# Norms of q and k and the softmax's inverse sums by way of DRAM, in a two-layer hybrid diffusion block

## The chip, the cores and the metric

The kernel runs on one core of a Trainium2 chip. A core has a matrix engine (TensorE, PE in the profile), three engines that work element by element (VectorE or DVE, ScalarE or ACT, GpSimd or POOL), and SyncE (SP), which here does nothing but issue DMA transfers. Each engine has its own list of instructions and works through it in order; semaphores hold an instruction back until what it needs is done. The metric is the device time of one execution, in microseconds (us).

## What is computed

Two layers work on 256 context tokens followed by 256 latent tokens, 1024 features wide. Each layer norms its input, projects it to the inputs of three branches (a state-space branch, SSD; neighbourhood attention; a gated MLP), sums the gated branches, projects, and ends with a SwiGLU block. The last layer returns the latent tokens only. The parts that matter here are the norm of q and k per head and the softmax:

```
def qkv_heads(t, q_norm, k_norm):
    q, k, v = [u.reshape(Bt, L, NA_HEADS, NA_HEAD_DIM) for u in split_cols(t, (NA_WIDTH,) * 3)]
    return rmsnorm(q, q_norm), rmsnorm(k, k_norm), v          # 8 heads of 64
...
    p = jax.nn.softmax(jnp.concatenate([s_lat, s_ctx], axis=3).astype(jnp.float32), axis=3)
    out = einsum(p_lat, v_win) + einsum(p_ctx, vc)            # latent queries
    ...
    p = jax.nn.softmax(s.astype(jnp.float32), axis=-1)        # context queries, layer 0 only
```

## The kernel before

Activations lie with features on the 128 partitions and the 512 tokens along the free dimension (context in columns 0 to 255, latent in 256 to 511). Layer 1 needs the context only for k, v and the SSD states, so most of its products are 256 columns wide.

Weights are streamed once, in the order of use, in 316 loads of 512 KB (tile `wr`, five buffers shared with another stream, `wm`). For each, ACT makes a high part (`hi`, L222) and DVE the remainder (`lo`, L232), and every product is three matmuls: high by high, high by low, low by high. A load is issued by SP once DVE has made the low part that frees its buffer.

All work is written in one fixed order by hand. The products of the weights are the main line; each of them calls `tick`, and at each tick three queues of side work (`ssd`, `att`, `mod`) move one or more steps forward (one `yield` of a generator is a step). `later(dt, fn)` puts a piece of work off by dt ticks. So the order of every engine, SP's too, is fixed when the program is built, and a wait of an instruction holds everything behind it on its engine.

`qk_norm` runs in the `att` queue, four times: k and q in each layer. The squares of four tiles (two heads in each) are summed by heads with a small matmul into 32 rows for each of the four tiles; ACT takes the root, DVE inverts it (`rq`, two halves), a high and a low part are put into `RQ`, and for each tile a matmul with a constant selector (`selp`) spreads two heads' rows over 64 partitions each, into PSUM. DVE multiplies q or k by it (L1094). Between these stand fixed numbers of steps: Q_0, Q_1 and Q_2.

`attention` follows in the same queue. For each head, `scores_lat` or `scores_ctx` makes the scores, their maximum, and on ACT the exponentials with their sums (`bt` for latent queries, two tiles of 128x512; `pc` for context queries, two halves of 128x256). Half a tick later DVE inverts the sums and scales the exponentials (L1148 to L1150, L1169 to L1172). Two steps after its scores a head's probabilities are transposed on PE (`transp`, L1186), and four steps after them `pv_out` multiplies two heads by v, and ACT and DVE split the result into `yna` (tiles `ynh`, `ynl`; `ynp` in layer 1; L1202, L1203). There are 16 such heads in layer 0 (8 of the context, 8 of the latent tokens) and 8 in layer 1.

The SSD branch already sends small rows through DRAM: `Fd` and `Cd` are stored from `R`, and `fetch` loads two rows of `Fd`, repeated on all partitions, into `rb`, from which DVE makes a mask `M` one step later (L896).

Of the kernel before, what the change touches and what calls it, by code (L numbers as in the profile page):

```python
# [33 lines left out]
C_ROW = 1280  # L34
# [61 lines left out]
def kernel(ctx: ExitStack, tc: tile.TileContext, a, out):  # L96
# [19 lines left out]
    def T(s="t", dt=F32):  # L116
        return tpool.tile([128, TOK], dt, tag="t", name=nm(s))

    def S(s="s"):
        return pspool.tile([128, 512], F32, tag="p", name=nm(s))  # L120
# [25 lines left out]
    selp = cpool.tile([128, 8, 128], F32R, name="selp")  # L146
    lom = cpool.tile([128, 1], F32, name="lom")
# [227 lines left out]
    def table(func):  # L375

        ACT.activation(dummy, epsb, func)
# [227 lines left out]
    for l in range(NL):  # L605
# [39 lines left out]
        if not last:  # L645
            SP.dma_start(out=cst[:, 0:C_ONE], in_=a["cst"][:, 0:C_ONE])
            SP.dma_start(out=cst[:, C_COS:C_ROW], in_=a["cst"][:, C_COS:C_ROW])
            SP.dma_start(out=cst[:, C_BS:C_MF], in_=a["cst"][:, C_BS:C_MF])
            SP.dma_start(out=mk, in_=a["cst"][:, C_MF:NC_])
            DVE.tensor_copy(selp.rearrange("p a (b c) -> p a b c", c=64),  # L650
                            cst[:, C_SP:C_SP + 16].rearrange("p (a b) -> p a b", b=2).unsqueeze(3).to_broadcast(
                                [128, 8, 2, 64]))

            DVE.tensor_reduce(out=lom, in_=cst[:, C_ROW + 4:C_ROW + 8], op=ADD, axis=AX.X)
            DVE.tensor_scalar(lom, lom, -1.0, None, MUL)
# [119 lines left out]

        def pair_rows(j, pr):

            return selp[:, 2 * j + pr]
# [287 lines left out]
        def qk_norm(kind):  # L1066
# [7 lines left out]
            rq, RQ = T("rq"), T("RQ", F32R)  # L1074
            if kind == "q":
                ACT.activation(rq[:, b:], ps[:, b:], AF.Sqrt, bias=eps64)
            else:
                ACT.activation(rq[:, b:], ps[:, b:], AF.Sqrt, scale=1.0 / 64, bias=epsb)
            table(AF.Exp)
            for c in range(b, 512, 256):  # L1080
                DVE.reciprocal(rq[:, c:c + 256], rq[:, c:c + 256])
                yield
            for _ in range(Q_1[l]):
                yield

            ACT.copy(RQ[:, b:], rq[:, b:])
            DVE.scalar_tensor_tensor(RQ[:, b:], RQ[:, b:].bitcast(F32), lom, rq[:, b:], MUL, ADD)
            for _ in range(Q_2[l]):
                yield
            for j in range(4):  # L1090
                ps = S()
                mm(ps[:, b:], pair_rows(j, 0), RQ[:, b:])
                t = qk[kind, j]
                DVE.scalar_tensor_tensor(t[:, b:], t[:, b:], pcol(P_KN if kind == "k" else P_QN),  # L1094
                                         ps[:, b:], MUL, MUL)
                yield

        def attention():
# [34 lines left out]

            def scores_lat(hd):
# [12 lines left out]
                def rest():  # L1147
                    DVE.reciprocal(st_[:, 6:8], st_[:, 4:6])  # L1148
                    for qt in (0, 1):
                        DVE.tensor_scalar(pr[qt], pr[qt], st_[:, 6 + qt:7 + qt], None, MUL)  # L1150

                later(A_N[l], rest)
                return pr

            def scores_ctx(hd):
# [12 lines left out]
                def rest():  # L1168
                    DVE.reciprocal(st_[:, 6:8], st_[:, 4:6])  # L1169
                    for qt in (0, 1):  # L1170
                        sl = slice(qt * 256, qt * 256 + 256)
                        DVE.tensor_scalar(p[:, sl], p[:, sl], st_[:, 6 + qt:7 + qt], None, MUL)  # L1172

                later(A_N[l], rest)
# [17 lines left out]
            def pv_out(s_, j, pts):  # L1192
# [9 lines left out]
                ACT.copy(hi[:, sl], ps[:, 0:256])  # L1202
                DVE.tensor_tensor(lo[:, sl], ps[:, 0:256], hi[:, sl], SUB)  # L1203
# [484 lines left out]
```

## Time and profile before

| | |
|---|---|
| median of 3 runs | 1604.22 us (1604.22 to 1604.6) |
| the profiled execution, its own time | 1605.74 us |
| its span, from the first instruction to the last | 1603.7 us |
| TensorE busy | 1581.2 us |
| DVE busy | 1162.3 us |
| ACT busy | 830.3 us |
| granted TensorE clock, mean | 0.997 of full speed |

Busy times are those of the engines' instructions; ends of matmuls are modelled, so that TensorE's figure also covers some time in which it is not at its peak. SP's work is the issue of transfers and is not counted.

### The profile page before, as it was taken

To read this page: it belongs to the slowest core of one execution; us is meant where nothing else is said; L and a number is where in the kernel's file an instruction comes from. 1 tells how busy PE (TensorE), PEld (TensorE's weight loads), DVE (VectorE), ACT (ScalarE), POOL (GpSimd) and SP (SyncE) were. 2 spreads that over 40 slices of the span, in tenths; PEclk is the share of its full clock that TensorE was granted. 3 is DMA by queue.
4 is the path that set the end of the run, shared out by engine and by line. 5 is a ranking of instruction groups with operands and counts; after the bars stand their busy time and mean duration, and the time that the engine had idled before them with its cause. 6 is when DMAs were issued, how large, how long until landed. Compare 5 with 4: busy or idle time off the path is not lost.

```text
span 1603.7 us, 23594 instructions
## 1 busy us (share of the span) xinstructions
PE 1581.2 (99%) x8908; PEld 1324.2 (83%) x8909; DVE 1162.3 (72%) x2005; ACT 830.3 (52%) x1551; POOL 6.9 (0%) x21
## 2 busy tenths in 40 slices
PE   9999999999999999999999999999999999999999
PEld 5878787767788888988888888978888989998888
DVE  5477889878968656666666654778988987687664
ACT  4456876646743234433222212658676775566652
POOL 0000000000000000000000000000000000000000
PEclk9999999999999999999999999999999999999999
DMA  9523333443344445455456765425434455656654
GB/s 347 190 61 122 115 107 107 154 153 99 113 130 127 157 144 178 133 171 166 162 184 206 261 231 177 171 93 161 132 118 138 140 158 178 204 163 196 187 173 135
DMA packets 87345, 254.37 MB, mean 159 GB/s; under 512 B 10560, under 2 KB 19008, under 8 KB 87104
## 3 DMA queue, kind: packets, MB, share of 16 engines
q1 hardware_dynamic: 87232, 252.87, 49.3%
q8 instruction: 70, 1.15, 0.3%
q14 instruction: 43, 0.35, 0.1%
HBM read 248.44 MB, written 4.39 MB: 158 GB/s over the span
## 4 chain that ended last, share of the span: by engine, by line
PE 78%; DVE 11%; ACT 5%; DMA 4%; issue 2%; SPq 0%; ACTq 0%; DVEq 0%
PE g L126 70%; PE s L126 6%; DVE lo L232 3%; DVE xbc L718 2%; DMA wm<-in_wmod 1%; ACT hi L222 1%; DMA rb<-Fd 1%; PE s L1186 1%; ACT M L987 1%; DVE scr L192 1%; DMA wr<-in_ws 1%; DVE bt L1141 0%; DVE M L896 0%; ACT rb L987 0%; ACT sw L740 0%
## 5 line engine op out<-in xcount | busy, mean ns | idle before, releaser
L126 PE MATMUL g<-hh,hi 128*128 128x512 f32 (+1 forms) x1280 | 471.0, 368 | 0.0
L126 PE MATMUL g<-hh,lo 128*128 128x512 f32 (+1 forms) x1280 | 462.0, 361 | 1.4 <-DVE lo L232 1.4
L126 PE MATMUL g<-hl,hi 128*128 128x512 f32 (+1 forms) x1280 | 461.8, 361 | 0.5 <-DVE hl L551 0.4
L232 DVE TENSOR_TENSOR lo<-wr,hi 128x1024 fp32r<-128x1024 f32 x316 | 382.5, 1219 | 92.9 <-ACT hi L222 92.7
L222 ACT CAST hi<-wr 128x1024 fp32r<-128x1024 f32 x316 | 323.7, 1046 | 38.8 <-DMA wr<-in_ws 36.0
L126 PEld LDWEIGHTS g<-hh,hi 128*128 128x128 f32 x1280 | 241.5, 189 | 48.7 <-issue 11.9
L126 PEld LDWEIGHTS g<-hh,lo 128*128 128x128 f32 x1280 | 241.5, 189 | 41.1 <-DVE lo L232 3.8
L126 PEld LDWEIGHTS g<-hl,hi 128*128 128x128 f32 x1280 | 241.7, 189 | 37.2 <-DVE hl L551 1.1
L192 DVE SCALAR_TENSOR_TENSOR scr<-wm,csil 128x1024 bf16<-128x1024 f32 x128 | 156.1, 1220 | 55.4 <-DMA wm<-in_wmod 55.4
L126 PE MATMUL g<-hp,hi 128*128 128x512 f32 x304 | 107.6, 399 | 0.0
L718 DVE SCALAR_TENSOR_TENSOR xbc<-g,pv,xbc 128x508 f32<-128x508 f32 (+3 forms) x128 | 91.3, 713 | 9.5 <-ACT xbc L712 6.4
L126 PE MATMUL g<-hp,lo 128*128 128x256 f32 x304 | 85.6, 282 | 0.9 <-DVE lo L232 0.8
L1295 ACT ACTIVATE th<-g,pv 128x512 f32<-128x512 f32 (+1 forms) x48 | 27.9, 581 | 95.3 <-PE g L126 89.6
L367 ACT CAST fh<-f 128x512 fp32r<-128x512 f32 x22 | 13.6, 620 | 112.3 <-DVE f L1446 112.3
L126 PE MATMUL g<-fh,lo 128*128 128x512 f32 x176 | 68.6, 390 | 0.5 <-DVE lo L232 0.5
L126 PEld LDWEIGHTS g<-hp,hi 128*128 128x128 f32 x304 | 57.1, 188 | 14.1
L126 PE MATMUL g<-fh,hi 128*128 128x512 f32 x176 | 68.5, 389 | 0.0
L126 PE MATMUL g<-fl,hi 128*128 128x512 f32 x176 | 68.5, 389 | 0.0
L126 PE MATMUL g<-lo,hh 128*128 128x256 f32 x224 | 63.6, 284 | 3.2 <-DVE lo L232 3.1
L126 PE MATMUL g<-hi,hh 128*128 128x256 f32 x224 | 64.6, 288 | 0.0
L126 PE MATMUL g<-hi,hl 128*128 128x256 f32 x224 | 63.3, 283 | 0.0
L126 PE MATMUL g<-fp,hi 128*128 128x512 f32 (+1 forms) x198 | 62.4, 373 | 0.0
(310 smaller groups left out, 2658.2 us busy)
## 6 DMA issues: line engine op xcount, KB each, us to landing
wr<-in_ws SPq DMA_DIRECT2D x316, 512.0 KB, 4.2
wm<-in_wmod SPq DMA_DIRECT2D x80, 512.0 KB, 4.5
rb<-Fd SPq DMA_DIRECT2D x48, 256.0 KB, 4.0
wm<-in_wm SPq DMA_DIRECT2D x32, 256.0 KB, 6.0
ex<-Cd SPq DMA_DIRECT2D x32, 128.0 KB, 3.8
bias<-in_rpb SPq DMA_DIRECT2D x32, 128.0 KB, 2.1
x<-in_xT SPq DMA_DIRECT2D x8, 256.0 KB, 5.1
xm<-in_xT SPq DMA_DIRECT2D x8, 256.0 KB, 5.5
```

Of the source, the lines that this page charges most:

```text
L126: PE.matmul(o, l, r, start=start, stop=stop)
L192: DVE.scalar_tensor_tensor(scr, raws[n], 1.0, csil[:, v, :], MUL, MUL, accum_out=modr[l][:, ft, v:v + 1])
L222: ACT.copy(hi, self.raw[i])
L232: DVE.tensor_tensor(lo, self.raw.pop(i), hi, SUB)
L367: ACT.copy(hi, src[:, c0:])
L718: DVE.scalar_tensor_tensor(av3[:, :, o0:o1], pv3[:, :, o0 + d:o1 + d], w(j), av3[:, :, o0:o1], MUL, ADD)
L987: ACT.activation(z, z, AF.Exp, bias=bias(st, d))
L1186: PE.transpose(ps[:, kt * 256 + qt * 128:kt * 256 + qt * 128 + 128], src, ident)
L1295: ACT.activation(th[:, c0:], ps[:, c0:], AF.Tanh, scale=0.5, bias=pcol(P_BG + br * 8 + m))
```

## The change

In the norms, the summed squares are copied out of PSUM as they are, and the two useful rows of each tile are stored to DRAM (`Nd`, four stores). They come back laid out over all 128 partitions, 32 numbers in each (`rqs`; 16 for q in layer 1), are rooted and inverted there, go to DRAM again, and are loaded for each tile, every row repeated on 64 partitions (`RQ`, two loads by `spread`). DVE multiplies by that tile in SBUF. The selector matmuls, the constant `selp` and the splitting are gone; the two steps between the halves of the reciprocal are gone too.

In attention, the inverse sums of a head (two numbers on each of 128 partitions) are stored to DRAM by `inverse` (tile `Pd`, one row of 256 numbers), and loaded back as a row repeated on 64 partitions (`inv`). The probabilities stay as they are; `pv_out` multiplies the heads' outputs by `inv`, and splits that product.

```diff
@@ -143,8 +143,6 @@
...
-    selp = cpool.tile([128, 8, 128], F32R, name="selp")
-    lom = cpool.tile([128, 1], F32, name="lom")
...
@@ -647,12 +645,6 @@
-            DVE.tensor_copy(selp.rearrange("p a (b c) -> p a b c", c=64),
-                            cst[:, C_SP:C_SP + 16].rearrange("p (a b) -> p a b", b=2).unsqueeze(3).to_broadcast(
-                                [128, 8, 2, 64]))
-
-            DVE.tensor_reduce(out=lom, in_=cst[:, C_ROW + 4:C_ROW + 8], op=ADD, axis=AX.X)
-            DVE.tensor_scalar(lom, lom, -1.0, None, MUL)
@@ -1071,28 +1059,42 @@
             ps = S()
             for j in range(4):
                 mm(ps[32 * j:32 * j + 32, b:], cst[:, C_BS:C_BS + 32], qsq.pop((kind, j))[:, b:])
-            rq, RQ = T("rq"), T("RQ", F32R)
-            if kind == "q":
-                ACT.activation(rq[:, b:], ps[:, b:], AF.Sqrt, bias=eps64)
-            else:
-                ACT.activation(rq[:, b:], ps[:, b:], AF.Sqrt, scale=1.0 / 64, bias=epsb)
-            table(AF.Exp)
-            for c in range(b, 512, 256):
-                DVE.reciprocal(rq[:, c:c + 256], rq[:, c:c + 256])
-                yield
+
+            n = 512 - b
+            t, w = T("rq"), small(32, "rqs", 2)
+            Nd, Ni = (dpool.tile([8, n], F32, name=nm("Nd")) for _ in range(2))
+            ACT.copy(t[:, b:], ps[:, b:])
+            for j in range(4):
+                SP.dma_start(out=Nd[2 * j:2 * j + 2], in_=t[32 * j:32 * j + 2, b:])
+            flat = lambda z: z.rearrange("h t -> (h t)").rearrange("(p c) -> p c", p=128)
+            w = w[:, 0:n // 16]
+            SP.dma_start(out=w, in_=flat(Nd))
             for _ in range(Q_1[l]):
                 yield
-
-            ACT.copy(RQ[:, b:], rq[:, b:])
-            DVE.scalar_tensor_tensor(RQ[:, b:], RQ[:, b:].bitcast(F32), lom, rq[:, b:], MUL, ADD)
+            if kind == "q":
+                ACT.activation(w, w, AF.Sqrt, bias=eps64)
+            else:
+                ACT.activation(w, w, AF.Sqrt, scale=1.0 / 64, bias=epsb)
+            table(AF.Exp)
+            DVE.reciprocal(w, w)
+            SP.dma_start(out=flat(Ni), in_=w)
+            R = {}
+
+            def spread(j):
+                R[j] = T("RQ")
+                for a_ in (0, 1):
+                    SP.dma_start(out=R[j][64 * a_:64 * a_ + 64, b:],
+                                 in_=Ni[2 * j + a_].unsqueeze(0).to_broadcast([64, n]))
+
+            spread(0)
             for _ in range(Q_2[l]):
                 yield
             for j in range(4):
-                ps = S()
-                mm(ps[:, b:], pair_rows(j, 0), RQ[:, b:])
                 t = qk[kind, j]
+                if j < 3:
+                    spread(j + 1)
                 DVE.scalar_tensor_tensor(t[:, b:], t[:, b:], pcol(P_KN if kind == "k" else P_QN),
-                                         ps[:, b:], MUL, MUL)
+                                         R.pop(j)[:, b:], MUL, MUL)
                 yield
 
         def attention():
@@ -1130,6 +1132,19 @@
                 Q, lo, K = st[hd]
                 mm(ps, Q[:, q0:q0 + 128], K[:, 0:n], True, False)
                 mm(ps, lo[:, q0:q0 + 128], K[:, 0:n], False, True)
+
+            Pd = dpool.tile([16, 256], F32, name=nm("Pd"))
+            inv = {}
+
+            def inverse(s_, hd, st_):
+
+                DVE.reciprocal(st_[:, 6:8], st_[:, 4:6])
+                j, q = divmod(hd, 2)
+                if q == 0:
+                    inv[s_, j] = small(256, "inv", 3)
+                row = Pd[s_ * 8 + hd]
+                SP.dma_start(out=row.rearrange("(q p) -> p q", p=128), in_=st_[:, 6:8])
+                SP.dma_start(out=inv[s_, j][64 * q:64 * q + 64, :], in_=row.unsqueeze(0).to_broadcast([64, 256]))
 
             def scores_lat(hd):
                 pr = []
@@ -1144,12 +1159,7 @@
                     ACT.activation(bt, bt, AF.Exp, bias=st_[:, 2 + qt:3 + qt], accum_out=st_[:, 4 + qt:5 + qt])
                     pr.append(bt)
 
-                def rest():
-                    DVE.reciprocal(st_[:, 6:8], st_[:, 4:6])
-                    for qt in (0, 1):
-                        DVE.tensor_scalar(pr[qt], pr[qt], st_[:, 6 + qt:7 + qt], None, MUL)
-
-                later(A_N[l], rest)
+                later(A_N[l], lambda: inverse(1, hd, st_))
                 return pr
 
             def scores_ctx(hd):
@@ -1165,13 +1175,7 @@
                     ACT.activation(p[:, sl], ps[:, sl], AF.Exp, bias=st_[:, 2 + qt:3 + qt],
                                    accum_out=st_[:, 4 + qt:5 + qt])
 
-                def rest():
-                    DVE.reciprocal(st_[:, 6:8], st_[:, 4:6])
-                    for qt in (0, 1):
-                        sl = slice(qt * 256, qt * 256 + 256)
-                        DVE.tensor_scalar(p[:, sl], p[:, sl], st_[:, 6 + qt:7 + qt], None, MUL)
-
-                later(A_N[l], rest)
+                later(A_N[l], lambda: inverse(0, hd, st_))
                 return p
 
             def transp(s_, pr):
@@ -1199,8 +1203,10 @@
                            pts[q][kt // 2][:, (kt % 2) * 256:(kt % 2) * 256 + 256], kt == 0, kt == nk - 1)
                 hi, lo, b = yna[j]
                 sl = slice(s_ * 256 - b, s_ * 256 + 256 - b)
-                ACT.copy(hi[:, sl], ps[:, 0:256])
-                DVE.tensor_tensor(lo[:, sl], ps[:, 0:256], hi[:, sl], SUB)
+                y = inv.pop((s_, j))
+                DVE.tensor_tensor(y, y, ps[:, 0:256], MUL)
+                ACT.copy(hi[:, sl], y)
+                DVE.tensor_tensor(lo[:, sl], y, hi[:, sl], SUB)
 
             items = [(j, s_, q) for j in range(4) for s_ in ((1,) if last else (0, 1)) for q in (0, 1)]
             pr, pts = {}, {}
```

How this moves the instructions is seen at three places. The names are those of the tiles, with a number that tells buffers apart; line numbers differ by a few between the two programs, and L230 and L210 of the changed one are L232 and L212 of the one before. First DVE in the attention of layer 0, around the end of the fifth head and the first heads' output. Before:

```order
L232 TENSOR_TENSOR lo_3582<-wr_3396,hi_3581 128x1024
L1169 RECIPROCAL ast_3616<-ast_3616 128x2
L1172 TENSOR_SCALAR pc_3624<-pc_3624,ast_3616 128x256 x2
L1203 TENSOR_TENSOR ynl_3647<-s_3648,ynh_3646 128x256
L1160 TENSOR_REDUCE ast_3669<-s_3670 128x2
L1161 TENSOR_SCALAR ast_3669<-ast_3669 128x2
L1331 SCALAR_TENSOR_TENSOR z_3686<-z_3686,g_3580 128x512
```

And with the change:

```order
L230 TENSOR_TENSOR lo_3600<-wr_3412,hi_3599 128x1024
L1141 RECIPROCAL ast_3634<-ast_3634 128x2
L1207 TENSOR_TENSOR inv_3456<-inv_3456,s_3667 128x256
L1209 TENSOR_TENSOR ynl_3666<-inv_3456,ynh_3665 128x256
L1170 TENSOR_REDUCE ast_3689<-s_3690 128x2
L1171 TENSOR_SCALAR ast_3689<-ast_3689 128x2
L1337 SCALAR_TENSOR_TENSOR z_3706<-z_3706,g_3598 128x512
```

The two scalings of `pc` are gone, a multiplication by `inv` has come, and the subtraction of `ynl` now reads `inv` and, through ACT's cast, depends on that multiplication.

Second SP in layer 0, from the weights' loads ahead of the norm of k to the first rows of the SSD branch. Before:

```order
L212 DMA wr_1367<-in_ws 128x1024
L212 DMA wr_1415<-in_ws 128x1024
L869 DMA Fd_625<-R_1431 64x128 x2
L871 DMA Cd_626<-R_1431 16x128 x4
L888 DMA rb_1440<-Fd_625 128x512
L888 DMA rb_1442<-Fd_625 128x512
L212 DMA wr_1488<-in_ws 128x1024
L212 DMA wr_1551<-in_ws 128x1024
```

And with the change:

```order
L210 DMA wr_1362<-in_ws 128x1024
L1068 DMA Nd_1380<-rq_1378 2x512 x4
L1071 DMA rqs_1379<-Nd_1380 128x32
L210 DMA wr_1414<-in_ws 128x1024
L857 DMA Fd_620<-R_1430 64x128 x2
L859 DMA Cd_621<-R_1430 16x128 x4
L876 DMA rb_1439<-Fd_620 128x512
L876 DMA rb_1441<-Fd_620 128x512
L1080 DMA Nd_1381<-rqs_1379 128x32
L1086 DMA RQ_1487<-Nd_1381 64x512 x2
L210 DMA wr_1494<-in_ws 128x1024
L210 DMA wr_1555<-in_ws 128x1024
```

Stores and loads of the norm (`Nd`, `rqs`, `RQ`) stand among the weights' loads (`wr`) and the rows of the SSD branch (`Fd`, `Cd`, `rb`): one weight's load now stands behind the load of `rqs`, and two behind the first `RQ`.

Third DVE in layer 0, ahead of two low parts of weights in the middle of the multiplications of q. Before:

```order
L1005 SCALAR_TENSOR_TENSOR xbc_1801<-xbc_1801,pv_176,s_2325 128x256
L993 TENSOR_TENSOR rb_2195<-M_2235 128x2x128
L994 TENSOR_TENSOR rb_2195<-rb_2195,cb_2043 128x512
L1017 TENSOR_TENSOR ex_2232<-ex_2232,s_2298 128x512
L896 TENSOR_TENSOR M_2337<-rb_2290,mk 128x512
L1094 SCALAR_TENSOR_TENSOR q_1444<-q_1444,pv_176,s_2347 128x512
L232 TENSOR_TENSOR lo_2306<-wr_2055,hi_2305 128x1024
L993 TENSOR_TENSOR rb_2237<-M_2288 128x2x128
L994 TENSOR_TENSOR rb_2237<-rb_2237,cb_2043 128x512
L896 TENSOR_TENSOR M_2369<-rb_2339,mk 128x512
L1094 SCALAR_TENSOR_TENSOR q_1577<-q_1577,pv_176,s_2383 128x512
L232 TENSOR_TENSOR lo_2390<-wr_2207,hi_2389 128x1024
```

And with the change, from two multiplications earlier on:

```order
L1096 SCALAR_TENSOR_TENSOR q_1581<-q_1581,pv_174,RQ_2283 128x512
L722 SCALAR_TENSOR_TENSOR xbc_2259<-ct_2302,xbc_2259 128x512
L710 SCALAR_TENSOR_TENSOR xbc_2324<-g_2261,pv_174,xbc_2324 128x2x254
L710 SCALAR_TENSOR_TENSOR xbc_2324<-g_2261,pv_174,xbc_2324 128x2x255 x2
L710 SCALAR_TENSOR_TENSOR xbc_2324<-g_2261,pv_174,xbc_2324 128x2x254
L993 SCALAR_TENSOR_TENSOR xbc_1812<-xbc_1812,pv_174,s_2347 128x256
L981 TENSOR_TENSOR rb_2209<-M_2249 128x2x128
L982 TENSOR_TENSOR rb_2209<-rb_2209,cb_2052 128x512
L1005 TENSOR_TENSOR ex_2246<-ex_2246,s_2316 128x512
L884 TENSOR_TENSOR M_2359<-rb_2308,mk 128x512
L1096 SCALAR_TENSOR_TENSOR q_1733<-q_1733,pv_174,RQ_2320 128x512
L230 TENSOR_TENSOR lo_2328<-wr_2071,hi_2327 128x1024
```

Ahead of the low part that is `lo_2306` before and `lo_2328` now stood one multiplication of q, `q_1444`. Now `q_1443`, `q_1581` and `q_1733` stand ahead of it, the first of them just above these rows.

## Rows read from the trace of the kernel before

**Rows 1.** The page, busy time (share of the span) and instructions.

```profile
PE 1581.2 (99%) x8908; PEld 1324.2 (83%) x8909; DVE 1162.3 (72%) x2005; ACT 830.3 (52%) x1551; POOL 6.9 (0%) x21
```

**Rows 2.** The page, chain that ended last, shares by engine.

```profile
PE 78%; DVE 11%; ACT 5%; DMA 4%; issue 2%; SPq 0%; ACTq 0%; DVEq 0%
```

**Rows 3.** Chain in order of time: start us, us, what; layer 0.

```profile
448.14 8.19 PE g L126 x36
```

**Rows 4.** Windows of the four stretches: length, then busy us (instructions) by engine.

```profile
core 0: us, PE busy (x) PEld busy (x) DVE busy (x) ACT busy (x) POOL busy (x), PEclk, DMA share, GB/s
130.00:275.00 145.00, 140.54 (x739) 111.55 (x738) 126.17 (x205) 104.70 (x235) 0.00 (x0) 1.00 0.38 117
340.00:470.00 130.00, 125.78 (x649) 97.19 (x648) 111.84 (x234) 80.13 (x166) 4.25 (x9) 1.00 0.38 120
1080.00:1215.00 135.00, 132.09 (x792) 111.60 (x791) 120.65 (x205) 96.46 (x208) 0.00 (x0) 1.00 0.42 128
1245.00:1320.00 75.00, 74.03 (x580) 66.62 (x579) 64.57 (x148) 56.77 (x116) 2.15 (x7) 1.00 0.49 148
```

**Rows 5.** Tiles rq and RQ: ns min/median/max, first and last start us, forms.

```profile
L1081 DVE RECIPROCAL rq<-rq x7: 1741/1744/1753, 140.5 to 1165.1; 128x256 f32<-128x256 f32 x7
...
L126 PE MATMUL s<-RQ,selp x16: 278/486/580, 176.5 to 1206.2; 128*128 128x512 f32 x12, 128*128 128x256 f32 x4
...
L1087 DVE SCALAR_TENSOR_TENSOR RQ<-RQ,lom,rq x4: 476/742/752, 158.4 to 1186.1; 128x512 fp32r<-128x512 f32 x3, 128x256 fp32r<-128x256 f32 x1
```

**Rows 6.** Tiles ast (the first two rows) and ynh, same columns.

```profile
L1150 DVE TENSOR_SCALAR bt<-bt,ast x32: 477/484/490, 374.6 to 1303.8; 128x512 f32<-128x512 f32 x32
...
L1172 DVE TENSOR_SCALAR pc<-pc,ast x16: 335/352/677, 362.9 to 436.6; 128x256 f32<-128x256 f32 x16
...
L1203 DVE TENSOR_TENSOR ynl<-s,ynh x8: 411/416/426, 384.4 to 458.7; 128x256 fp32r<-128x256 f32 x8
```

**Rows 7.** Timeline of DVE and PE: start us, us, what, [idle before <- releaser].

```profile
242.98 0.74 DVE L1094 SCALAR_TENSOR_TENSOR q<-q,pv,s 128x512 f32<-128x512 f32 x1
...
243.64 1.22 DVE L232 TENSOR_TENSOR lo<-wr,hi 128x1024 fp32r<-128x1024 f32 x1
...
244.91 0.38 PE L126 MATMUL g<-lo,hh 128*128 128x256 f32 x1 [2.18 <-DVE lo L232]
...
253.23 0.47 PE L126 MATMUL s<-RQ,selp 128*128 128x512 f32 x1 [1.34 <-DVE xbc L718]
```

**Rows 8.** Waits, 340:470 and 1245:1320 (last row): us, times, longest.

```profile
PE s L1186 <- DVE bt L1150: 1.1, 2, 0.6
PE s L1186 <- DVE pc L1172: 1.0, 1, 1.0
...
PE s L1186 <- DVE z L1331: 0.7, 2, 0.5
```

**Rows 9.** Tile rb: one of its instructions, and its loads' landing.

```profile
L896 DVE TENSOR_TENSOR M<-rb,mk x48: 681/684/693, 160.2 to 1237.9; 128x512 f32<-128x512 f32 x48
...
DMA to landing us min/median/max: 3.0/4.0/8.4
```

**Rows 10.** Waits of the whole run, same columns as rows 8.

```profile
DVE M L896 <- DMA rb<-Fd: 5.7, 3, 2.0
```

**Rows 11.** Timeline of DVE: first and last of four multiplications of k.

```profile
181.52 0.74 DVE L1094 SCALAR_TENSOR_TENSOR k<-k,pv,s 128x512 f32<-128x512 f32 x1
...
196.05 0.74 DVE L1094 SCALAR_TENSOR_TENSOR k<-k,pv,s 128x512 f32<-128x512 f32 x1
```

**Rows 12.** DMA issues: count, KB each, median us to landing.

```profile
wr<-in_ws SPq DMA_DIRECT2D x316, 512.0 KB, 4.2
...
Cd<-R SPq DMA_DIRECT2D x8, 8.0 KB, 1.5
```

**Rows 13.** Timeline of SP and ACT: a load's issue and its cast, layer 1.

```profile
1285.01 0.43 SPq L212 DMA_DIRECT2D wr<-in_ws  x1
...
1291.20 7.18 SPq L212 DMA_DIRECT2D wr<-in_ws  x4
...
1298.29 1.04 ACT L222 CAST hi<-wr 128x1024 fp32r<-128x1024 f32 x1
```

More of the change, by code (lines that the diff above doesn't have):

```diff
@@ L774 @@
         Cd = dpool.tile([16, 4, 128], F32, name=nm("Cd"))
-        def pair_rows(j, pr):
-            return selp[:, 2 * j + pr]
         def dt_gen():
```

## The prediction

> **What bounds the kernel now.** I read the page's busy line first: TensorE is busy 99% of the span [rows 1]. A busy PE there is not proof of a PE bound, since ends of matmuls are modelled, so I went on to the chain that ended last: 78% of it is PE, 11% VectorE (DVE), 5% ScalarE (ACT), 4% DMA [rows 2]. The chain's pieces give PE's pace: 36 matmuls of 512 columns in 8.19 us, 0.2275 us each [rows 3]; I take half of that, 0.114, for 256 columns. PE works through one long, fixed list, and what counts is how long it stands still between two items. The change touches four stretches: the norms of layer 0 (130 to 275 us), its attention (340 to 470), and the same in layer 1 (1080 to 1215, 1245 to 1320). There PE is busy 140.54 of 145, 125.78 of 130, 132.09 of 135 and 74.03 of 75 us [rows 4]: 12.6 us idle in all. So removed waits can give at most some 12.6 us, and removed PE work comes on top. DVE is busy 126.17 and 111.84 us in the first two: no spare engine, at some places it is the one that PE waits for.
>
> **What the change removes, part by part.**
>
> Matmuls. The sixteen that spread the inverse roots, twelve of 512 columns and four of 256 [rows 5], go: 12 x 0.2275 + 4 x 0.114 = 3.2 us of PE. That is the whole of PE's direct gain, and just 0.2% of the time.
>
> DVE in the norms. Seven reciprocals of 128x256 at 1.744 us, 12.2 us, and four splits into a high and a low part, 3 x 0.74 + 0.48 = 2.7 us [rows 5], go. In their place stand four reciprocals of 128x32 or 128x16, together under 1 us (an eighth of a 1.744 is 0.22). The eight multiplications of k and the eight of q keep their size; they read SBUF and not PSUM, which I cost at nothing.
>
> ACT in the norms. The two table loads, the root and the dummy stay in number; the wide root becomes a plain copy of its width, a root of 32 columns is added, the wide cast goes. I cost the difference at zero. But the table loads move some steps later, to where ACT also makes the decay weights.
>
> DVE in attention. 32 scalings of 128x512 at 0.484 us and 16 of 128x256 at 0.352 us go [rows 6], 21.1 us. Twelve multiplications of 128x256 come; the nearest row is the subtraction of that size out of PSUM, 0.42 us [rows 6], so 5 us. Net 16 us less.
>
> DMA. Each norm adds 4 stores, a load, a store and 8 spreading loads, 56 in the four norms; each head adds a store of 256 single numbers and a load, 48 in 24 heads. All are issued by SP, in the fixed order of the second order fence above, with the weights' loads behind them.
>
> **What that is worth on PE.** (a) Matmuls in the norms of layer 0. At 244.91 us PE had waited 2.18 us for a weight's low part, which DVE began at 243.64, right behind the first multiplication of q [rows 7]. In the new order three multiplications of q stand ahead of that low part instead of one (third pair of order fences); each holds DVE 0.66 us (242.98 to 243.64), so 1.3 us more, against 0.74 for the split that is gone: it comes about 0.6 us later. PE gets there earlier by the six matmuls removed ahead of it, 1.4 us, and waits that much longer. So of 3.2 us I count 3.2 - 1.4 - 0.6 = 1.2. Bounds: 0, and 3.2 if the two reciprocals gone before that place let DVE arrive early. (b) At 253.23 us the spreading matmul itself waited 1.34 us for a PSUM buffer that a convolution still read [rows 7]; the matmul is gone, but the next user of a PSUM buffer may inherit the wait. Half: 0.7; bounds 0 and 1.34. (c) Attention of layer 0: the transposes waited 1.1 us for scaled probabilities of the latent tokens and 1.0 us for those of the context [rows 8]. They will wait for the exponentials alone, done earlier: 2.1 us. In layer 1, two waits of transposes behind DVE's backlog, 0.7 us [rows 8], go too. Bounds for (c): 0, and all of PE's idle time in the two attention stretches, 5.2 us [rows 4]. (d) 16 us less of DVE work in attention shortens other small waits on it: 0.5 (0 to 2.4, what is left of the 5.2).
>
> **What it costs.** The norms' loads: the spreading load for the next pair of heads is issued one step ahead. Existing loads of the same kind, rb from Fd, are fetched so that the mask a step later reads them; they take 4.0 us in the median, 8.4 at most, and DVE waited for one only 3 times, 5.7 us in all, out of 48 [rows 9, 10]. Steps lie some 4.8 us apart on DVE (four multiplications of k, the first at 181.52, the last at 196.05 [rows 11]). A split load costs one more issue, some 0.5 us. So it mostly lands in time: 0 in the median, and up to 12 x 1 us of DVE waits, below the 14.9 us that DVE is relieved of there.
>
> The heads' round trip: store, landing, load, landing. Nearest rows: a store of 8 KB, Cd<-R, lands in 1.5 us [rows 12]; for the load of 64 KB I take the 4.0 us of rb [rows 9] as the upper end. With two issues of some 0.4 us that is 6.3 us after the reciprocal. It is needed three and a half steps later. A step in layer 0 is 5.6 us: the first scaling of pc starts at 362.9, the last, half of a head, at 436.6 [rows 6], 13 heads on, and (73.7 - 0.4)/13 = 5.6. So there are 19 us for it: hidden, cost nothing. While SP waits for the store to land, everything behind it waits too, 1.5 + 0.8 = 2.3 us per head. The weights' loads have room: the one issued at 1285.01 us is cast at 1298.29 [rows 13], and a load takes 4.2 us to land [rows 12], so 9 us of slack against 2.3. Zero. The bound is the rival below.
>
> A page bears on that store. The Trainium skill, DMA: Bandwidth & Descriptors, Rules for kernel authors, says that a strided or non-contiguous last dimension becomes one descriptor for each element, and advises rearranging so that it is contiguous. The store of a head's sums puts neighbouring partitions' numbers side by side, so by that rule it is 256 descriptors of 4 bytes. No run here has such a store yet; by the rule it should take longer than the 1.5 us above, and only from about 6 us would the sum change.
>
> At each head pair DVE multiplies, ACT then casts, DVE then subtracts: ACT now waits for DVE and DVE for ACT. At every second head this takes back about what the two scalings of a context head gave: 0.42 for the multiplication, and a change of engine for which I have no row, against 2 x 0.352 [rows 6]. At the end of layer 1's attention the last pair has no cover: I add 0.5 us.
>
> **Sum.** -1.2 - 0.7 - 2.8 - 0.5 + 0.5 = -4.7 us. The profiled execution takes 1605.74 us and would take 1601.0; the runs shown have a median of 1604.22, 1.5 lower, so I forecast 1599.5 us.
>
> **Rivals.** *Nothing to measure* (less than 0.2% either way, about what this kernel's measurement can tell from no change, 3.2 us): DVE and ACT set the pace in both norm stretches, as at 244.91, and all matmul gains wait there; only (c) is left, or is lost to the new DVE-ACT turn: 1601.5 to 1604. Against it: layer 1's norms show 2.9 us idle in 135 [rows 4], and (b) is PE's own wait for a buffer, not for DVE.
>
> *More than forecast*: DVE's relief removes most of the 12.6 us idle: -3.2 and some -6, 1595.
>
> *The small store holds SP* (slower). With landing time L, SP is held L + 0.8 us per head. Steps are 5.6 us in layer 0 and about 6.2 in layer 1 (loads at 1285.01 and 1291.20 [rows 13]); beyond that the delay adds up over 16 and 8 heads, less 9 us slack each. At L = 8.4 us (the longest row of a landing [rows 9]): 16 x 3.6 + 8 x 3.0 - 18 = 64 us, 1663. It decides from L of about 5.8 us. For it: nothing so fine-grained is in the trace. Against: a store of a few KB takes 1.5. This is the way that the Trainium skill's rule named above points.
>
> *The spreading loads come late* (slower). Three loads in each norm that wait 2 us cost DVE 24 us, 9 more than it was relieved of: 1604.2 - 2.8 (the attention's part, (c), (d) and the 0.5 behind) + 9 = 1610. It decides from 14.9/12 = 1.2 us each. Against it: the 3 waits out of 48 [rows 10].
>
> **How the numbers follow.** Forecast 0.50 (1597 to 1601), more than forecast 0.12, nothing to measure 0.20, small store 0.09, late loads 0.09. Faster by over 0.2%: 0.62; within: 0.20; slower: 0.18. The forecast's own range is 1597 to 1601. For 8 in 10 I go from 1592.5, which is the matmuls and two thirds of the idle time (3.2 + 8.5), to 1606, which takes in the whole of the second case and loads that come a little late.
>
> **What would show it.** Right: no wait of transposes on a scaling; PE's idle time in the stretch that is 340 to 470 now down from 4.2 to about 2 us; no ACT wait on a weight's load in the four stretches; inverse-sum stores landing in 2 to 3 us; the wait at 244.91 still there, longer. Wrong: stores over 5 us, ACT's casts waiting for weights, DVE's multiplications of q or k waiting for their load, or ACT's roots waiting for theirs.

## The result: 8.6% slower, and the profile after

The changed kernel takes 1742.68 us in the median (1739.89 to 1744.76), the kernel before on the same chip 1604.41: a ratio of 1.0861 [1.0847, 1.0874], 138 us more. The forecast was 1599.5 us with a range to 1606; what happened is in the main the rival "the small store holds SP", which had 9 chances in 100, and it came larger than worked out there (1663).

The page of the changed kernel, busy time and the chain that ended last:

```profile
PE 1609.9 (93%) x8892; PEld 1343.7 (77%) x8893; DVE 1135.8 (65%) x1959; ACT 830.7 (48%) x1551; POOL 6.9 (0%) x21
...
PE 70%; DMA 14%; DVE 7%; ACT 4%; SPq 2%; issue 2%; DVEq 0%; ACTq 0%
PE g L126 65%; DMA Pd<-ast 10%; PE s L126 4%; DMA wr<-in_ws 2%; DVE lo L230 2%; DVE xbc L710 1%; DMA rb<-Fd 1%; ACT hi L220 1%; ACT M L975 1%; SPq L1129 1%; DMA wm<-in_wmod 1%; DVE M L884 0%; SPq L1147 0%; SPq L210 0%; DMA x<-in_xT 0%
```

Against [rows 1, 2] the PE's share has fallen from 99% to 93%, and DMA's share of the chain has risen from 4% to 14%. One transfer alone, the store of a head's inverse sums `Pd`, holds 10% of the chain. The four stretches of [rows 4], found again by the casts of the same weights (times between two casts are interpolated), in the changed kernel:

```profile
131.50:280.60 149.10, 140.75 (x731) 111.58 (x730) 118.87 (x201) 104.53 (x235) 0.00 (x0) 0.98 0.41 129
345.80:556.10 210.30, 141.72 (x646) 107.13 (x645) 100.75 (x207) 80.72 (x166) 4.27 (x9) 0.82 0.33 75
1166.10:1309.60 143.50, 134.10 (x784) 113.03 (x783) 115.81 (x202) 96.54 (x208) 0.00 (x0) 0.98 0.45 132
1339.60:1455.50 115.90, 84.83 (x577) 73.43 (x577) 60.00 (x136) 56.75 (x116) 2.15 (x7) 0.86 0.35 98
```

Their lengths have grown by 4.1, 80.3, 8.5 and 40.9 us, 133.8 in sum. The spans of the two profiled executions differ by 1738.0 - 1603.7 = 134.3, so all of the loss lies here, 121 of it in the two attentions. PE's idle time in them went from 12.6 us to 117.4; the other 29 us are PE's busy time, which is longer where the granted clock is lower (0.82 and 0.86 in the attentions, 1.00 before). DVE's busy time fell by 28 us, close to the 31 of the forecast, and bought nothing.

The SP timeline of the changed kernel in the attention of layer 0 shows the wait:

```profile
368.71 0.38 SPq L1146 DMA_DIRECT2D Pd<-ast  x1
377.10 0.45 SPq L1147 DMA_DIRECT2D inv<-Pd  x1
...
379.30 0.96 SPq L1146 DMA_DIRECT2D Pd<-ast  x1
389.50 0.45 SPq L1147 DMA_DIRECT2D inv<-Pd  x1
...
392.09 0.38 SPq L1146 DMA_DIRECT2D Pd<-ast  x1
401.12 0.45 SPq L1147 DMA_DIRECT2D inv<-Pd  x1
```

From the store's issue to the issue of the load that needs it, 8.39, 10.20 and 9.03 us pass, and SP stands for nearly all of that time. The store of 8 KB in [rows 12] took 1.5. With what else SP has to issue, a head takes it 10.6 and 12.8 us here, against a step of 5.6 us before: SP sets the pace of the attention (between 340 and 560 us the landing of these stores is 59% of the chain). In the first of these waits hardly anything is moved (the window of 369.20 to 377.00, DMA share 0.02):

```profile
369.20:377.00 7.80, 7.80 (x41) 6.44 (x40) 5.63 (x15) 4.89 (x11) 1.04 (x2) 1.00 0.02 0
```

What waited in the end (waits of the whole run: us, times, longest). Before:

```profile
DVE scr L192 <- DMA wm<-in_wmod: 55.4, 26, 4.0
...
ACT hi L222 <- DMA wr<-in_ws: 36.0, 16, 5.9
...
PE g L126 <- DVE lo L232: 6.7, 9, 2.2
```

And with the change:

```profile
DVE scr L190 <- DMA wm<-in_wmod: 139.2, 33, 21.3
...
ACT hi L220 <- DMA wr<-in_ws: 59.4, 18, 11.0
...
PE g L126 <- DVE lo L230: 38.6, 15, 10.4
...
PE s L126 <- DVE z L1337: 36.0, 2, 20.7
```

SP issues the loads late. The wait that grew most, by 84 us, is DVE's for `wm`, the second stream of weights, which DVE multiplies in `scr`; ACT's wait for `wr` grew by 23. What stands behind `scr` in DVE's order is late with it, such as `z`, which DVE begins at 440.96 us, and PE waits for that (timelines of DVE and PE):

```profile
439.81 1.23 DVE L190 SCALAR_TENSOR_TENSOR scr<-wm,csil 128x1024 bf16<-128x1024 f32 x1 [17.84 <-DMA wm<-in_wmod]
...
441.70 0.80 PE L126 MATMUL s<-ks,qs 128*128 128x512 f32 x1 [15.36 <-DVE z L1337]
```

### The profile page after: what moved, and what is told of

The parts are those of the page before. It is cut to its first block, busy times and chain, and to the rows that moved or that the text cites. A ratio compares the mean times of both kernels' runs of the same rounds, so it can differ in the third digit from the quotient of the medians.

```text
span 1738.0 us, 23731 instructions
## 1 busy us (share of the span) xinstructions
PE 1609.9 (93%) x8892; PEld 1343.7 (77%) x8893; DVE 1135.8 (65%) x1959; ACT 830.7 (48%) x1551; POOL 6.9 (0%) x21
## 4 chain that ended last, share of the span: by engine, by line
PE 70%; DMA 14%; DVE 7%; ACT 4%; SPq 2%; issue 2%; DVEq 0%; ACTq 0%
PE g L126 65%; DMA Pd<-ast 10%; PE s L126 4%; DMA wr<-in_ws 2%; DVE lo L230 2%; DVE xbc L710 1%; DMA rb<-Fd 1%; ACT hi L220 1%; ACT M L975 1%; SPq L1129 1%; DMA wm<-in_wmod 1%; DVE M L884 0%; SPq L1147 0%; SPq L210 0%; DMA x<-in_xT 0%
## 5 line engine op out<-in xcount | busy, mean ns | idle before, releaser
L126 PE MATMUL g<-hh,hi 128*128 128x512 f32 (+1 forms) x1280 | 481.7, 376 | 17.5 <-DVE z L1337 7.5
L126 PE MATMUL g<-hh,lo 128*128 128x512 f32 (+1 forms) x1280 | 470.5, 368 | 25.5 <-DVE lo L230 25.5
L126 PE MATMUL g<-hl,hi 128*128 128x512 f32 (+1 forms) x1280 | 470.0, 367 | 0.5 <-DVE hl L549 0.4
L230 DVE TENSOR_TENSOR lo<-wr,hi 128x1024 fp32r<-128x1024 f32 x316 | 382.5, 1219 | 98.8 <-ACT hi L220 98.3
L126 PEld LDWEIGHTS g<-hh,hi 128*128 128x128 f32 x1280 | 247.7, 194 | 70.0 <-issue 20.4
L126 PEld LDWEIGHTS g<-hh,lo 128*128 128x128 f32 x1280 | 247.6, 193 | 68.0 <-DVE lo L230 29.4
L126 PEld LDWEIGHTS g<-hl,hi 128*128 128x128 f32 x1280 | 248.0, 194 | 37.9 <-DVE hl L549 1.1
L126 PE MATMUL g<-lo,hh 128*128 128x256 f32 x224 | 65.0, 290 | 10.6 <-DVE lo L230 10.6
L126 PE MATMUL s<-ks,qs 128*128 128x512 f32 (+1 forms) x48 | 20.7, 436 | 52.5 <-DVE z L1337 36.0
```

Of the source, the lines that this page charges most:

```text
L126: PE.matmul(o, l, r, start=start, stop=stop)
L230: DVE.tensor_tensor(lo, self.raw.pop(i), hi, SUB)
```

## The experiments

Each ratio is to the kernel before on the same chip. Differences are of medians; where it matters that two runs were on different chips, the difference by the ratios stands beside it.

**Which part loses.** e1_norms has the change in `qk_norm` alone, with the `attention` of before.

> The norms' part of the change alone, attention as before. Theory one (the loss is a store of single numbers that holds SP, so it is in attention): the norms have no such store; by the marks of the changed kernel's trace they lost some 12 us (the cast of the 36th weight stands 4 us further behind that of before than the 18th's, the 198th's 8 us further than the 174th's), so 1613 to 1619 us, with waits of PE for a low part near 250 us. Rival (the norms' 56 transfers are the source, and attention only inherits late weights): 1700 us or more. If attention's state spoils nothing backwards and the forecast's view of the norms was right: 1602 us.

Measured 1618.17 us, 1.0092 [1.0075, 1.0109]. So the norms lose 14 us, and the attention the other 124.5.

**Is it SP standing still?** e4_defer is the changed kernel with one line changed ("..." shortens it):

```
-                SP.dma_start(out=inv[s_, j][64 * q:64 * q + 64, :], in_=row...)
+                later(2.0, lambda: SP.dma_start(out=inv[s_, j][64 * q:64 * q + 64, :], in_=row...))
```

> The changed kernel, but the load of a head's inverse sums is issued two ticks later than its store, so that SP does not stand waiting while the store lands; the store itself and all arithmetic are unchanged. Theory one (what costs is SP held in order): the attention's 123 us go, the norms' 12 stay: 1612 to 1622. Rival (the store of 256 pieces itself clogs the queues, so that weights land late whoever waits): 1700 or more. Second rival (the DVE-ACT-DVE turn): 1735 to 1745.

Measured 1666.95, 1.0401 [1.0381, 1.0422]: 76 us of the 124.5 come back, and 49 do not. This is neither theory as put. Two ticks do not free SP: its waits for the store (the waits of SP's queue, first in the changed kernel, then in e4_defer) fell to a quarter, not to nothing.

```profile
SPq L1147 <- DMA Pd<-ast: 207.9, 24, 10.1
```

```profile
SPq L1147 <- DMA Pd<-ast: 53.1, 12, 7.6
```

ACT's wait for `wr` is back at what it was before (36.2 us against 36.0). What is new among the waits of e4_defer is DVE's for the loads of `inv`:

```profile
DVE inv L1208 <- DMA inv<-Pd: 34.3, 5, 11.2
```

The load behind the longest of these waits was issued 0.4 us after the store of another head, at 479.40 us, and DVE's multiplication by it began at 491.87. So the store may delay what is queued behind it; this run alone does not show it.

**Fewer pieces.** e3_pairs stores 128 pieces of 8 bytes instead of 256 of 4, and the outputs are multiplied and split in that order; SP waits as in the changed kernel:

```
-                SP.dma_start(out=row.rearrange("(q p) -> p q", p=128), in_=st_[:, 6:8])
+                SP.dma_start(out=row.rearrange("(p q) -> p q", q=2), in_=st_[:, 6:8])
```

> The changed kernel, but a head's inverse sums lie in DRAM with the two numbers of a partition side by side: 128 pieces of 8 bytes instead of 256 of 4; the load is as before, and the multiplication and the split read and write in that order. Theory one (the landing is paid by the piece: about 7.2 us pass after the last of 256 pieces has been sent, 28 ns each): SP is held some 4 to 5 us a head less than the step of 5.6 us, so most of the attention's 123 us goes: 1615 to 1650. Rival (a store of scattered small pieces has a fixed landing of 7 to 10 us): still 1735 to 1745. Second rival (the loss is the DVE-ACT-DVE turn of the new outputs): 1740 or a little more, since that turn is unchanged.

Measured 1653.19, 1.0307 [1.0287, 1.0328]: just past the 1650 that theory one allowed, far from both rivals. SP's waits for the store make 114.3 us here and 35 us of the attention's loss are left; e4_defer has 53.1 us of such waits and 49 us left. So SP's standing is not all of the loss.

**Few pieces.** e6_row turns the inverse sums (`w[:, 0:2]`) on DVE and stores 8 rows of 128 bytes:

```
+                DVE.transpose(out=w[:, 32:64], in_=w[:, 0:32])
...
+                for qt in (0, 1):
+                    SP.dma_start(out=row[qt * 128:qt * 128 + 128].rearrange("(b p) -> b p", p=32),
+                                 in_=w.rearrange("(b p) c -> p b c", p=32)[qt, :, 32:64])
```

> The changed kernel, but DVE turns a head's inverse sums with one 32x32 transposition of 128x32 (tile turn), so that they are stored as 8 pieces of 128 bytes in two transfers instead of 256 pieces of 4 bytes; SP waits for the landing as in the changed kernel, and the outputs are multiplied as there. Theory one (the landing and the queues are paid by the number of pieces; 256 pieces hold SP 7 to 10 us and hold the transfers behind them besides): both fall away, and the norms' loss stays: 1612 to 1624, stores landing in 2 to 3 us. Rival (a round trip by DRAM with SP waiting costs about the same for any layout, 7 us): 1720 or more. Second rival (the DVE-ACT-DVE turn is a good part of it): 1640 or more.

Measured 1615.0, 1.006 [1.004, 1.0079], 3.2 us below e1_norms (by the ratios 5; their intervals just overlap). All of the attention's loss is gone and there may be a small gain. SP still waits for every head's stores, only shorter, 43.7 us in all; its SP timeline:

```profile
370.34 1.12 SPq L1156 DMA_DIRECT2D Pd<-turn  x2
372.55 0.48 SPq L1146 DMA_DIRECT2D inv<-Pd  x1
```

2.2 us from the first of the two stores to the load. The DVE-ACT-DVE turn of the outputs, unchanged here, is therefore no part of the loss that can be seen.

**What makes the store slow.** e7_micro has stores alone, three of each form, and loads of 512 KB behind some of them. It ran once.

> Stores by themselves; nothing of the reference is computed and the outputs are zeros. Each store is followed by a load of one number of it, and the time from its issue to the issue of that load is its landing; three of each form. Theory one (a landing is paid by the piece below some size): 256 pieces of 4 bytes about 8 us, 128 of 8 or of 4 about half as much over a base of 1.5 to 2, 8 of 128 and 2 of 512 near the base. Rival one (what costs is that neighbouring small pieces fall into the same line of memory, one after another): 256 pieces 64 or 512 bytes apart land near the base. Rival two (fixed price of a small scattered store): 128 pieces as slow as 256. Then a weight's load of 512 KB alone, and right behind such stores: if the pieces hold the queues, the load behind 256 pieces lands several us later than alone, behind 2 pieces not.

Its SP timeline; L123 is 256 pieces of 4 bytes side by side, L128 128 of 8, L133 128 of 4, L138 8 of 128, L143 2 of 512, L148 and L153 256 pieces of 4 bytes that lie 64 and 512 bytes apart, L163 256 pieces of 64 bytes side by side; L170 is the load that waits for the landing:

```profile
28.70 0.36 SPq L123 DMA_DIRECT2D row<-src  x1
37.19 0.23 SPq L170 DMA_DIRECT2D back<-row  x1
40.64 0.33 SPq L128 DMA_DIRECT2D row<-src  x1
43.45 0.23 SPq L170 DMA_DIRECT2D back<-row  x1
...
67.65 0.33 SPq L133 DMA_DIRECT2D row<-src  x1
75.82 0.23 SPq L170 DMA_DIRECT2D back<-row  x1
...
92.76 0.26 SPq L138 DMA_DIRECT2D row<-src  x1
93.99 0.21 SPq L170 DMA_DIRECT2D back<-row  x1
...
108.92 0.39 SPq L148 DMA_DIRECT2D apart<-src  x1
110.54 0.21 SPq L170 DMA_DIRECT2D back<-apart  x1
...
133.16 0.39 SPq L163 DMA_DIRECT2D full<-src  x1
134.82 0.21 SPq L170 DMA_DIRECT2D back<-full  x1
```

8.49 us for the store of the changed kernel (8.06 in a second; the first, behind a store of 1 MB, 11.59), 1.62 for the same 256 pieces from the same place 64 bytes apart: so theory one falls, and rival one holds as far as it names the neighbours. It is not the number of pieces: 128 pieces of 4 bytes side by side take 8.17 (7.8 to 8.2 in three), as long as 256. Pieces of 8 bytes side by side, half as many to the same stretch of memory, take 2.81 (2.8 to 4.0 in three), 8 rows of 128 bytes 1.23. And it is only small neighbours: 256 pieces of 64 bytes side by side take 1.66. Why small neighbouring pieces are slow is not shown by these rows, only that they are.

Then a DVE copy of the weight as soon as it has landed (timeline of DVE; the issues on SP were at 141.24, 145.39, 149.68 and 176.96):

```profile
144.92 0.17 DVE L116 COPY src<-wr 128x8 f32<-128x8 f32 x1 [2.50 <-DMA wr<-in_ws]
149.05 0.17 DVE L116 COPY src<-wr 128x8 f32<-128x8 f32 x1 [3.96 <-DMA wr<-in_ws]
162.35 0.17 DVE L116 COPY src<-wr 128x8 f32<-128x8 f32 x1 [13.13 <-DMA wr<-in_ws]
...
180.88 0.17 DVE L116 COPY src<-wr 128x8 f32<-128x8 f32 x1 [4.41 <-DMA wr<-in_ws]
```

The load takes 3.68 us alone, 3.66 behind the store of 2 pieces, 12.67 behind the 256 neighbours, 3.92 behind the 256 pieces 64 bytes apart. So the slow store delays by 9 us what is issued right behind it, though SP does not wait here. With SP's 53.1 us of waits, that is what the runs offer for the 49 us left in e4_defer; how the 49 divide between the two is not shown.

**The norms.** e5_yields is e1_norms with the steps put back that fell away with the halves of the reciprocal, ahead of the root:

```
-            for _ in range(Q_1[l]):
+            for _ in range(Q_1[l] + n // 256):
```

> The norms' part alone as in e1_norms, with the steps that fell away with the halves of the reciprocal put back (two, one for q of layer 1), ahead of the root: the multiplications of k and q stand at the steps of before again. Theory one (the norms' loss is the order on DVE: multiplications that stand two steps earlier, ahead of weights' low parts that PE waits for): 1600 to 1605. Rival (the norms' loads come late, or SP is held by them, and the weights behind them are late): as e1_norms within 3 us.

Measured 1608.77, 1.0033 [1.002, 1.0046]: 9.4 of the 14 us. In layer 1 of e1_norms PE waited for low parts (its PE timeline):

```profile
1137.42 0.79 PE L126 MATMUL g<-hh,lo 128*128 128x512 f32 x1 [2.54 <-DVE lo L230]
...
1190.69 0.58 PE L126 MATMUL g<-lo,hh 128*128 128x256 f32 x1 [2.94 <-DVE lo L230]
```

In e5_yields these are 0.8 us and nothing, and the stretch of layer 1's norms takes 133.4 us against 135 in [rows 4] and 144.1 in e1_norms. So what the steps are worth lies in layer 1. The edit moves the root, its store, the loads and the multiplications together; which of them made PE wait is not separated. Layer 0's stretch is 149.5 still (149.2 in e1_norms), against 145. There SP had something new to wait for (SP timeline of e5_yields):

```profile
209.90 0.33 SPq L876 DMA_DIRECT2D rb<-Fd  x1
223.59 0.32 SPq L1080 DMA_DIRECT2D Nd<-rqs  x1
...
226.25 1.00 SPq L876 DMA_DIRECT2D rb<-Fd  x2
```

From 210.2 to 223.59 SP stands at the store of the roots, until they are made, with rows of the SSD branch and weights behind it. e8_pool is e5_yields with the norms' 56 transfers issued from GpSimd (`SP.dma_start` becomes `nc.gpsimd.dma_start` in the norm).

> As e5_yields (norms alone, with their steps put back), but the norms' stores and loads are issued by GpSimd's queue, not by SP. Theory one (what is left of the loss in layer 0, some 4 us near 225 us, is SP standing at the store of the roots, with the rows of the SSD branch and weights behind it): 1600 to 1605. Rival (it is the norms' loads' share of the transfers, or DVE's order): as e5_yields within 2 us.

Measured 1605.26, 1.0003 [0.999, 1.0015], just past theory one's upper end and 3.5 us below e5_yields (4.8 by the ratios), with intervals that do not touch; the rival allowed 2. Layer 0's stretch is 147.3 us. In it PE still waits 5.23 us near 248 us. On ACT the root's two table loads now stand among the decay weights (`rb`, `M`); timeline of ACT in e8_pool:

```profile
220.12 1.28 ACT L1075 ACT_TABLE_LOAD   x1
221.42 0.32 ACT L1075 ACTIVATE rqs<-rqs,eps 128x32 f32<-128x32 f32 x1
221.76 1.28 ACT L375 ACT_TABLE_LOAD   x1
```

In the kernel before, they stand where ACT waits for PE (its timeline of ACT):

```profile
192.38 1.28 ACT L1076 ACT_TABLE_LOAD   x1
196.00 0.69 ACT L1076 ACTIVATE rq<-s,eps 128x512 f32<-128x512 f32 x1 [2.33 <-PE s L126]
196.71 1.28 ACT L377 ACT_TABLE_LOAD   x1
```

e11_root puts the root back there, ahead of the first store:

```
-            ACT.copy(t[:, b:], ps[:, b:])
+            ACT.activation(t[:, b:], ps[:, b:], AF.Sqrt, ...)
+            table(AF.Exp)
...
-            ACT.activation(w, w, AF.Sqrt, ...)
-            table(AF.Exp)
             DVE.reciprocal(w, w)
```

> As e8_pool (norms alone, steps put back, their transfers by GpSimd's queue), but the root is taken where it was taken before the change, out of PSUM in place of the plain copy, so that its two table loads (1.28 us each) stand where ACT waits for PE anyway; only the reciprocal is left on the small tile. Theory one (what is left in layer 0, the wait of 5.2 us for a low part near 248 us, comes from the table loads in the middle of ACT's decay weights, some 3 us by which ACT and then DVE fall back): that wait is at 2.5 us or less and the time 1600 to 1603. Rival (DVE's relief falls where DVE then waits for PE, and the low part is late whatever ACT does): within 1.5 us of e8_pool, 1604 to 1606.

Measured 1603.78, 0.9998 [0.9989, 1.0007]. The wait near 248 us is halved, though not to the 2.5 us of theory one (PE timelines of e8_pool and then of e11_root):

```profile
248.05 0.58 PE L126 MATMUL g<-lo,hh 128*128 128x256 f32 x1 [5.23 <-DVE lo L230]
```

```profile
244.59 0.39 PE L126 MATMUL g<-lo,hh 128*128 128x256 f32 x1 [2.66 <-DVE lo L230]
```

and layer 0's stretch is 143.9 us, 3.4 less than in e8_pool and 1.1 less than before. But layer 1's is 135.1, where e8_pool had 133.3, so half of it is lost again. The wait and the stretch of layer 0 speak for theory one; in the total, 1.5 us, the intervals of the two overlap, the 1603 that I allowed as the upper end was missed, and the distance to e8_pool is one that the rival allowed. So the price of the table loads' place is read from one stretch of one execution of each kernel, not shown by the time.

e11b_rootsp is e11_root with SP as the issuer again.

> e11_root with the transfers on SP's queue again. Theory one (SP stood still at the store of the roots because the root came late; now it comes early, so SP is hardly held): within 2 us of e11_root. Rival (the norms' loads on SP's queue are the loss, whenever the root comes): 3 to 5 us more than e11_root.

Measured 1606.89, 1.0012 [1.0002, 1.0022], 3.1 us above e11_root (2.2 by the ratios, whose intervals overlap): nearer the rival, but not clear of theory one. The premise of theory one was wrong: DVE's reciprocal still stands at the later step, so SP still stands at the store of its result, issued at 222.01 us there.

**What the parts are worth.** e10_noscale leaves the inverse sums out.

> The kernel before without the reciprocals and the 48 scalings of the probabilities, and with nothing in their place (the outputs are not divided by the sums): what the attention's part could give at most. The forecast's terms (c) and (d) make 3.3 us: 1600 to 1602. Rival (DVE's backlog in attention is worth more than its visible waits): 1597 or less. If more than 3.3 is left over against e9_oldnorm_row, the outputs' new turn costs that.

Measured 1597.79, 0.9963 [0.9949, 0.9977]: 5.9 us is about the most that the attention's part could give; the time lies between the two theories, near the rival's. e9_oldnorm_row has the norms of before and the attention with rows, the load one tick after the store.

> The norms of before, and the attention of the changed kernel with the rows of e6_row (8 pieces of 128 bytes), the load one tick after the store, and inv and turn in one tile of the common ring. Theory one (the new attention is worth what it takes off DVE once its store is cheap): 1599 to 1604. Rival (the outputs' DVE-ACT-DVE turn and the transfers take all of it back): 1604 to 1612.

Measured 1602.1, 0.998 [0.997, 0.9989]: 3.2 us of these 5.9. e12_best has both parts with their costs taken out (e11_root's norms, e6_row's attention).

> The norms of e11_root and the attention of e6_row together: the whole of the change with its four costs taken out (pieces of 4 bytes, the steps that fell away, SP held at the root's store, table loads in a busy place). If the parts add up (attention -3, norms 0 to -4): 1597 to 1601. Rival (the parts share the same relief): 1601 to 1604.

Measured 1600.43, 0.9977 [0.9968, 0.9987]: faster than both kernels, by 3.7 us than the one before (interval 2.1 to 5.1). Beside e9_oldnorm_row it shows no gain of the norms that these intervals can tell from none.

## Why the prediction was wrong

**The step that failed** is the heads' round trip: "a store of 8 KB, Cd<-R, lands in 1.5 us", and from it "1.5 + 0.8 = 2.3 us per head" of SP and "Zero" for the weights. The store of single numbers was priced by a row of a store of another form. SP waited 207.9 us for the 24 stores, 8.7 us each in the mean and 10.1 at most, and the weights came late. The rival had the right place and about the right landing (8.4), and its point of decision (5.8) was passed; against it I set the 1.5 us once more, so that it got 9 chances in 100. The trace of before had no row of such a store, and the honest range would have held both ends at similar chances. Three things were missing in its 64 us. SP's other issues in a step make the head 10.6 to 12.8 us long in the rows above, not 9.2. The store delays the load behind it as well (9 us in e7_micro). And PE's busy time in the two attentions is 27 us longer (141.72 + 84.83 against 125.78 + 74.03), at a granted clock of 0.82 and 0.86 instead of 1.00. The rule named in the prediction pointed to the right store for a reason that the runs do not bear out by itself: the Trainium skill, DMA: Bandwidth & Descriptors, Rules for kernel authors, speaks of one descriptor for each element, but 256 single numbers 64 bytes apart, by that rule 256 descriptors too, land in 1.62 us. The same page's Specifications say that transfers under 512 bytes are done by reading, modifying and writing; by that, neighbours that share what is read might have to wait for one another. That would fit the 8.49 against 1.62 us only if much less than 512 bytes were shared, since 256 pieces of 64 bytes side by side land in 1.66; no run here shows the reading.

**(a) and (b), norms: -1.9 forecast, +14 measured.** Three steps failed. First, in (a), the two steps that fell away were counted as 1.3 us of DVE in layer 0 and as nothing in layer 1; put back, they give 9.4 us, all of it in layer 1's stretch. Second, "mostly lands in time": the loads did, but SP's wait for the producer of a store (13 us at 210 us) was not in the working; 2 to 5 us (e5_yields against e8_pool; e11b_rootsp against e11_root, not clear of noise). Third, ACT: "I cost the difference at zero. But the table loads move some steps later" named the cost and left it out; 3.4 us in layer 0's stretch, 1.5 us and not clear of noise in the time. The 3.2 us of matmuls are not seen in the time: layer 1's stretch in e5_yields is 1.6 us shorter than before, against 1.4 for its eight matmuls, but in e11_root it is not shorter at all. The wait at 244.91 is still there and longer, as forecast (5.70 us in the changed kernel).

**DVE's relief** (14.9 and 16 us) was sized well (28 us of 31 in the four stretches) and is worth little, as forecast.

**(c) and (d), attention: -2.8 with the 0.5 behind.** Right in size once the store is cheap: 3.2 us in e9_oldnorm_row (0.002 of 1604.9, interval 1.8 to 4.8), and the same in e6_row against e1_norms. The mechanism holds too: among PE's waits in e9_oldnorm_row none of a transpose on DVE is left, where [rows 8] have 2.8 us of them. The rival of late spreading loads did not happen: in the changed kernel no multiplication of q or k waits for its load.

## What to carry to other kernels

Before sending a column of single numbers through DRAM, turn it on chip so that the store writes rows: the same 1 KB lands in 1.2 to 2.2 us instead of 8 (e7_micro, e6_row). Rows of 512 bytes did not hold the load queued behind them (3.66 us against 3.68 alone). Price a transfer by a row of its own form, and where there is none, let the range hold both ends. When work moves by a few steps in fixed orders, look at all that moves with it: the steps that an edit deletes, the table loads, and the issuing engine that stands at a store until its producer is done.

## What the hardware showed that was not expected

The landing of small stores goes by neighbourhood: 8.17 us for 128 pieces of 4 bytes side by side, 8.49 for 256, 1.62 for 256 that lie 64 bytes apart. A load behind two such stores of 256 (issued at 163.53 us in e7_micro, landed by 176.30) takes 12.77 us, no longer than behind one (12.67). And a wait of PE is paid twice when the clock falls with it: PE stood still for 5.70 us in layer 0 of the changed kernel (the first row, timeline of PE), and from its next matmul until 255 us the granted clock is half, 1.2 of 2.4 GHz; its window row stands in the second fence (column PEclk):

```profile
250.85 0.58 PE L126 MATMUL g<-lo,hh 128*128 128x256 f32 x1 [5.70 <-DVE lo L230]
```

```profile
250.90:255.00 4.10, 4.10 (x19) 3.14 (x19) 4.07 (x6) 3.07 (x4) 0.00 (x0) 0.51 0.46 137
```
